# Second block: S5 pairs by couples, and the mixer norm and output product ahead of the S5 drain

## The chip, the cores and the metric

One core of one Trainium2 chip runs the whole program. The metric is device time in microseconds (us) of one execution, lower is better. Engines: PE (TensorE, matmuls), DVE (VectorE), ACT (ScalarE), POOL (GpSimd) and SP (which issues the loads). Each engine works through its own instructions in order; semaphores tie them together.

## The reference

256 tokens of width 1024 go through two blocks. The first (attention, short convolution, a large expert layer) isn't touched. The second puts 16 meta tokens ahead (272 positions in all) and computes:

```
h = layer_norm(concat([meta, x]))
p = h @ w_in + b_in                    # u_s5, q, k, v, o_pre, i_pre, f_pre, g_s5, g_m
# S5: 32 groups of 16 channels, 64 complex states each
state_t = lam_bar * state_(t-1) + b_bar @ u_t ;   y = Re(c @ state) + d * u
z = gelu(y_s5) @ s5_w_glu ;   y_s5 = z[:, :1024] * sigmoid(z[:, 1024:])
# mLSTM: 4 heads, running maximum, numerator over denominator
hm = head_norm(mlstm(silu(conv(q)), silu(conv(k)), v, i_pre, f_pre))
y_m = (sigmoid(o_pre) * hm) @ m_w_out
mix = sigmoid(g_s5) * y_s5 + sigmoid(g_m) * y_m
h = layer_norm(ALPHA * h + mix @ w_o)
out = layer_norm(ALPHA * h + relu(h @ w_up + b_up)^2 @ w_down)
```

## The kernel before, in words

Features stand on the 128 partitions, tokens on the columns. Large products are made in three: each weight tile (128 x 1024) is loaded, rounded to a high part `hi` by ACT (line 189), and its remainder `lo` is made by DVE (line 192); `mm3` (lines 212, 215, 216) multiplies hi by hi, hi by lo and lo by hi. A tile of the input projection (`project`, printed as `pj`) is 24 matmuls. There are three buffers of each of raw, hi and lo.

PSUM has four whole banks for tiles (`bank`), and four `single` banks. `s5_pair(p)` handles two of the 32 groups of S5, 16 pairs in all. Two input matmuls (`bu`, line 1665: real and imaginary part) use 32 rows of PE's array each; rows 32 x (p mod 4). DVE then turns them by the states' angles (six products, lines 1671 to 1676) and scans them (line 1680, `wr` and `wi`), and POOL turns them back (six products, lines 1683 to 1688, of which 1686, `wr`, is printed last). `s5_read(p)` makes the output, two matmuls (`s5y`, line 1699) on 32 columns of the array; four pairs fill one bank, and after the fourth DVE adds `d * u` (`s_y`), and ACT takes the gelu.

The mLSTM has per head `mlstm_head` (`negm`, `qk`, and the weights `m_e`) and `mlstm_sums` (`num`, line 1528, then the statistics `m_st` and `m_ag`). `mlstm_out` takes the denominators and variances of all heads (lines 1542 to 1551, with a root on ACT in `rsqrt`), norms the eight row tiles (four on ACT, line 1556, four on DVE, line 1561), turns them in 16 transposes (`hmT`, line 1571) and multiplies by the output gate (`yin_f`, line 1573).

S5 pairs, gate steps and heads aren't written where they run. They are put in a queue with a cost, `later(cost, fn)`; `pump(budget)`, called after each projection tile, takes items while the budget lasts, and `drain()` takes the rest. Budgets are P_V per tile of values and P_S per gate tile. A scheduler with its own time line then sets the order on each engine, by readiness and by the order of writing. In before the queue holds heads and S5 items mixed; 24 gate tiles (o, gs, gm; `sig0` to `sig2`) are projected with a pump each, then comes the drain, then `mlstm_out`, the gated unit (`glu`, eight tiles), the output product (`ym`, eight tiles) and `w_o`.

Of the kernel before, what the change touches and what calls it, by code (L numbers as in the profile page):

```python
# [18 lines left out]
T = 256  # L19
# [46 lines left out]
P_U, P_V, P_QK, P_S = 0.9, 2.5, 0.6, 2.4  # L66
# [10 lines left out]
K1, K1_BUFS = 272, 12  # L77
# [3 lines left out]
class K:  # L81
# [136 lines left out]
    def after(self, x, y):  # L218
        """The instruction x behind y in the order of their engine."""
# [3 lines left out]
    def rsqrt(self, v):  # L223
        """1 / sqrt(v), with a step of Newton's after the root."""
        nc, (p, n) = self.nc, v.shape
        r, t, h = (self.work(64, "rs_" + x, 3)[0:p, 0:n] for x in "rth")
# [11 lines left out]
    def rms_scale(self, ssq, n, width, eps):  # L238
        v = self.work(64, "rs_v", 3)[:, 0:n]
# [8 lines left out]
    def ln_scale(self, st, p=128):  # L248
        """mean and 1 / sd of rows, from the statistics of their halves."""
# [3 lines left out]
        v = self.work(64, "rs_v", 3)[0:p, 0:1]  # L253
# [3 lines left out]
    def transposed(self, xn, k):  # L257
        """The k-th 128 features of all tokens, in two halves of PSUM banks."""
# [72 lines left out]
    def silu_row_at_once(self, row):  # L331
        """The same with a small load: the tensor engine repeats the row."""
# [9 lines left out]
    def ada_col(self, m, f, ring=None, pool=False, paced=False):  # L342
        """The f-th column of the m-th vector, without its bias."""
# [13 lines left out]
    def ada_gate(self, m, g):  # L357
        """The m-th vector as a row on all partitions."""
# [16 lines left out]
    def modulation(self, m, norm, name, k=0, n=8):  # L375
        """Scale and shift of blocks k.. of the features; m is the vector of shifts, m + 1 that of scales."""
# [30 lines left out]
    def rms_rows(self, x, t, ssq, xn):  # L407
        """x -> x / rms, from the sums of the squares of quarters."""
        nc = self.nc
        s = self.work(64, "rs_s", 3)[:, 0:1]  # L410
# [9 lines left out]
    def add_gated(self, acc, gate, quarter, row):  # L420
        """x1 += acc * gate by quarters of the rows of t, with what follows each of them."""
# [132 lines left out]
    def qkv_load(self, i, per):  # L554
        """The i-th tile of weights of q, or of k and v: that many blocks of 128 features."""
# [19 lines left out]
    def conv_branch(self):  # L575
        """Features on partitions."""
# [351 lines left out]
    def ranks(self, t):  # L928
        """Places among the candidates -> ranks in the two lists that they were made of."""
# [59 lines left out]
    def expert_in(self, j):  # L989
        """The activations of experts j (mod 128); where the gates are there already, times those."""  # L990
# [15 lines left out]
    def gates(self, t0):  # L1006
        """The gates of 8 tokens: onto the activations that are there, and in the places of the others."""
# [48 lines left out]
    def sum_rows(self, acc, n, term, after=None, held=HELD):  # L1056
        """acc[t] = sum of n products; the last ones of t = 0 go before those of t = 1, and those by halves."""
# [43 lines left out]
    def open_lo(self):  # L1101
        """What the second block needs of its own, in the place of the first half of the experts."""
# [26 lines left out]
    def second_block(self):  # L1129
# [22 lines left out]
        for p in range(16):  # L1152
            self.later(2.8, self.s5_pair, p, u)
            if p:
                self.later(0, self.s5_read, p - 1, u)
            for step in steps[2 * p:2 * p + 2]:
                self.later(*step)
        self.later(0, self.s5_read, 15, u)
# [20 lines left out]
        while heads or rest:  # L1179
            for item in (heads.pop(0) if heads else []):  # L1180
                self.later(*item)
            self.queue.extend(rest[:4])
            rest = rest[4:]
        for n, name in enumerate(("b_o", "b_gs", "b_gm")):
            if n == 2:
                sig.append(cb([128, 8, L], "sig2")[:, :, 0:256])
            for c in range(8):
                b = self.project(20 + 8 * n + c, T)
                nc.scalar.activation(out=sig[n][:, c, :], in_=b, func=AF.Sigmoid, bias=self.vec(name, c))
                self.pump(P_S)  # L1190
# [90 lines left out]

    def lead_tiles(self, src):
# [46 lines left out]
    def add_residual(self, acc, h, row):  # L1329
        """x1 = ALPHA * h + acc, by halves of rows, with what follows the rows of t."""  # L1330
# [13 lines left out]
    def norm_row(self, t, st):  # L1344
        """(x - mean) / sd of the rows t of x1, in place of them."""
# [11 lines left out]
    def hold(self, x):  # L1357
        """The parts of the next tiles of weights that are taken on the vector engine come after x."""
# [55 lines left out]
    def if_gates(self):  # L1414
        """log i and log f of the four heads, and what the mixer needs of them, step by step."""
# [122 lines left out]
    def mlstm_out(self, rows, sig_o):  # L1538
# [13 lines left out]
        for h in range(4):  # L1552
            for t in range(2):
                i = 4 * t + h
                if h in NORM_ACT:
                    nc.scalar.activation(
                        out=rows[:, t, h, :], in_=rows[:, t, h, :], func=AF.Identity, scale=r[:, i:i + 1],
                        bias=nb[:, i:i + 1],
                    )
                    continue  # L1560
                nc.vector.tensor_scalar(
                    out=rows[:, t, h, :], in0=rows[:, t, h, :], scalar1=ag[:, i, 0:1], scalar2=r[:, i:i + 1],
                    op0=ALU.subtract, op1=ALU.mult,
                )
        self.tap("hm", rows)
        yin = self.ca([128, 2, 8, 256], "yin", F32R, tag="big", bufs=2)
        for c in range(8):
            b = self.bank("hmT")
            for t in range(2):
                e = (c % 2) * 128  # L1570
                nc.tensor.transpose(b[:, t * 128:t * 128 + 128], rows[:, t, c // 2, e:e + 128], self.ident)
            x = self.f256("yin_f")
            nc.vector.scalar_tensor_tensor(
                out=x, in0=b[:, 0:256], scalar=self.vec("mnorm_g", c), in1=sig_o[:, c, :],
                op0=ALU.mult, op1=ALU.mult,
            )
            self.split_into(yin[:, 0, c, :], yin[:, 1, c, :], x, YIN_ACT)
        return yin[:, 0], yin[:, 1]
# [18 lines left out]
    def s5_rates(self, free):  # L1597
# [12 lines left out]
        # (exp(lam dt) - 1) / lam  # L1610
# [16 lines left out]
        # the factor goes to the output's side: c * factor, its imaginary part negative  # L1627
# [13 lines left out]
    def s5_turns(self, p):  # L1641
        """cos and sin of the states' angles at each step."""
# [14 lines left out]
    def s5_pair(self, p, u):  # L1657
# [186 lines left out]
```

## Time and profile before

| | |
|---|---|
| runs | 1480.24, 1484.26, 1486.38 us; median 1484.26 |
| the profiled execution | span 1485.1 us, all that is timed of it, 0.8 us over the median |
| PE, DVE, ACT, POOL busy | 1418.8, 1129.7, 758.3, 144.7 us |
| loads from memory | 259.5 MB; a tile of 512 KB lands 3.5 us (median) behind its issue |
| chain that ended last | PE 78%, DVE 12%, ACT 4%, DMA 3% |
| the second block | from about 980 us to the end; S5 and mLSTM about 1020 to 1200 |

A row of the time line gives the start, the time from first to last of its instructions, the engine, line, operation, names (out<-in), partitions and columns, and their number; fp32 matmuls of S5 and mLSTM show as two instructions each. In brackets stands the idle time before it and the instruction that ended it. Matmuls overlap in the pipe, so the cost of one is read from its start to the next one's start. The table by stretches has PEclk, the granted clock of PE as a share of full speed.

### The profile page before, as it was taken

What the parts mean: (1) busy time and instruction counts of PE and PEld (TensorE: products, weight loads), DVE (VectorE), ACT (ScalarE), POOL (GpSimd) and SP (SyncE); (2) the same over time, 40 slices, a digit from 0 to 9 for tenths busy, and PEclk for the clock granted to TensorE, in tenths of its full rate; (3) what the DMA queues carried; (4) which work ended last, traced back from release to release, by engine and by line L of the source; (5) the groups of instructions that cost most, each with busy time, mean ns of one, the idle gap of its engine ahead of it and who ended that gap; (6) DMA issues with size and microseconds to landing.
All of it is one profiled execution on the core that took longest, in us unless ns stands there. A gap on an engine that the chain in (4) does not pass through costs nothing.

```text
span 1485.1 us, 24290 instructions
## 1 busy us (share of the span) xinstructions
PE 1418.8 (96%) x9217; PEld 1256.7 (85%) x9217; DVE 1129.7 (76%) x2330; ACT 758.3 (51%) x1292; POOL 144.7 (10%) x128
## 2 busy tenths in 40 slices
PE   6888999999999999999999999999899999999996
PEld 3776899999999999988887788878686799789995
DVE  7888799967788888665566688768799878675556
ACT  3365455544444444455445558745385474455552
POOL 0141000000000000000000000002756510000001
PEclk9998999999999999999999999999899999999999
DMA  9773446554444444555557685553232255366552
GB/s 383 293 267 114 171 149 195 194 174 153 146 139 146 143 146 146 172 189 185 190 192 243 216 270 194 186 187 129 85 128 95 96 193 186 113 200 201 195 186 99
DMA packets 72287, 263.20 MB, mean 177 GB/s; under 512 B 8149, under 2 KB 8533, under 8 KB 71786
## 3 DMA queue, kind: packets, MB, share of 16 engines
q1 hardware_dynamic: 72170, 261.66, 52.2%
q8 instruction: 72, 1.18, 0.3%
q14 instruction: 45, 0.37, 0.1%
HBM read 259.53 MB, written 2.10 MB: 176 GB/s over the span
## 4 chain that ended last, share of the span: by engine, by line
PE 78%; DVE 12%; ACT 4%; DMA 3%; issue 2%; POOL 1%; DVEq 0%; ACTq 0%; POOLq 0%
PE ea L216 8%; PE ea L212 8%; PE ea L215 8%; PE pe L215 7%; PE pe L216 7%; PE pe L212 7%; DVE lo L192 3%; PE gt L1021 2%; PE gt L1022 2%; PE ff L215 2%; PE ff L212 2%; PE ff L216 2%; PE up L216 2%; PE up L215 2%; PE up L212 2%
## 5 line engine op out<-in xcount | busy, mean ns | idle before, releaser
L189 ACT ACTIVATE hi<-raw 128x1024 fp32r<-128x1024 f32 x398 | 419.9, 1055 | 426.0 <-PE ea L215 108.4
L192 DVE TENSOR_TENSOR lo<-raw,hi 128x1024 fp32r<-128x1024 f32 x398 | 488.6, 1229 | 192.8 <-ACT hi L189 190.2
L212 PE MATMUL ea<-h,hi 128*128 128x256 f32 x1024 | 288.5, 282 | 0.8 <-ACT hi L189 0.8
L215 PE MATMUL ea<-h,hi 128*128 128x256 f32 x1024 | 289.1, 283 | 0.0
L216 PE MATMUL ea<-h,lo 128*128 128x256 f32 x1024 | 288.7, 283 | 0.0
L215 PE MATMUL pe<-lo,whi 128*128 128x512 f32 x512 | 201.0, 395 | 0.9 <-DVE lo L192 0.8
L216 PE MATMUL pe<-hi,wlo 128*128 128x512 f32 x512 | 199.0, 394 | 0.0
L212 PEld LDWEIGHTS ea<-h,hi 128*128 128x128 f32 x1024 | 193.7, 189 | 1.0 <-ACT hi L189 1.0
L216 PEld LDWEIGHTS ea<-h,lo 128*128 128x128 f32 x1024 | 193.5, 189 | 0.0
L215 PEld LDWEIGHTS ea<-h,hi 128*128 128x128 f32 x1024 | 193.4, 189 | 0.0
L212 PE MATMUL pe<-hi,whi 128*128 128x512 f32 x512 | 143.6, 395 | 1.1 <-ACT hi L189 1.0
L215 PEld LDWEIGHTS pe<-lo,whi 128*128 128x128 f32 x512 | 96.4, 188 | 24.7 <-DVE lo L192 2.6
L212 PEld LDWEIGHTS pe<-hi,whi 128*128 128x128 f32 x512 | 95.7, 188 | 23.8 <-ACT hi L189 2.2
L216 PEld LDWEIGHTS pe<-hi,wlo 128*128 128x128 f32 x512 | 96.4, 188 | 21.9
L212 PE MATMUL pj<-hT,hi 128*128 128x256 f32 (+1 forms) x328 | 97.6, 297 | 0.0
L215 PE MATMUL pj<-hT,hi 128*128 128x256 f32 (+1 forms) x328 | 95.0, 290 | 2.5 <-DVE hT L208 2.5
L216 PE MATMUL pj<-hT,lo 128*128 128x256 f32 (+1 forms) x328 | 94.4, 288 | 0.0
L212 PEld LDWEIGHTS pj<-hT,hi 128*128 128x128 f32 x328 | 63.6, 194 | 5.7 <-issue 1.9
L216 PE MATMUL up<-h1T,lo 128*128 128x256 f32 x240 | 66.9, 279 | 0.4 <-DVE lo L192 0.4
L212 PE MATMUL up<-h1T,hi 128*128 128x256 f32 x240 | 67.0, 279 | 0.2 <-ACT hi L189 0.2
L215 PE MATMUL up<-h1T,hi 128*128 128x256 f32 x240 | 66.8, 279 | 0.1
L215 PEld LDWEIGHTS pj<-hT,hi 128*128 128x128 f32 x328 | 63.5, 194 | 3.7 <-DVE hT L208 3.1
(471 smaller groups left out, 2765.9 us busy)
## 6 DMA issues: line engine op xcount, KB each, us to landing
raw<-in_u SPq DMA_DIRECT2D x128, 512.0 KB, 3.5
raw<-in_v SPq DMA_DIRECT2D x128, 512.0 KB, 3.5
raw<-in_sC SPq DMA_DIRECT2D x41, 512.0 KB, 3.5
raw<-in_down SPq DMA_DIRECT2D x32, 512.0 KB, 3.5
raw<-in_up SPq DMA_DIRECT2D x30, 512.0 KB, 3.5
s_hi<-in_ada SPq DMA_DIRECT2D x28, 512.0 KB, 5.7
raw<-in_sA SPq DMA_DIRECT2D x17, 512.0 KB, 4.3
s_hi<-in_sA SPq DMA_DIRECT2D x14, 512.0 KB, 6.2
```

Source lines behind the costliest of these rows:

```text
L189: self.last_hi = nc.scalar.activation(out=hi[:, 0:n], in_=raw[:, 0:n], func=AF.Copy)
L192: x = nc.vector.tensor_tensor(out=lo[:, 0:n], in0=raw[:, 0:n], in1=hi.bitcast(F32)[:, 0:n], op=ALU.subtract)
L212: i = mm(out, lhsT=w[0], rhs=x[0], start=first, stop=False)
L215: mm(out, lhsT=w[0], rhs=x[1], start=False, stop=False)
L216: return mm(out, lhsT=w[1], rhs=x[0], start=False, stop=last)
L1021: nc.tensor.matmul(b[:, i0 + i, :], lhsT=oa[:, :, i], rhs=ob[:, :, i], start=True, stop=False)
L1022: nc.tensor.matmul(b[:, i0 + i, :], lhsT=oa[:, :, i], rhs=oc[:, :, i], start=False, stop=True)
```

## The change

S5 goes by couples of pairs. `s5_in(p)` makes the four input matmuls of pairs p and p+1, real parts of both first, so that neighbours in the order use different rows of the array; it takes all four single banks. `s5_pair(p)` keeps only DVE's and POOL's part. `s5_read(p)` reads a couple, four matmuls on different columns. The order in the queue is in(p), pair(p), read(p-2), pair(p+1).

The heads are put ahead of what is left of S5 in the queue's mixture, with a mark behind the last head. After the 16 tiles of the gates o and gs the queue is pumped until the mark. Then comes the norm's scale; each of the eight gm tiles is followed by the norm of a head's rows (every second tile), two transposes and the split of `yin`, and the output product follows at once, with a pump per tile. The drain of S5 and the gated unit stand behind that. `mix` is now made at the end of the gated unit. `yin` takes two other buffers. Budgets change, 14 instead of 12 scratch tiles are used, and the scratch of `rsqrt` is narrower. No arithmetic goes or comes.

```diff
-P_U, P_V, P_QK, P_S = 0.9, 2.5, 0.6, 2.4
+P_U, P_V, P_QK, P_S, P_M = 0.9, 2.2, 0.6, 1.9, 1.9
-K1, K1_BUFS = 272, 12
+K1, K1_BUFS = 272, 14
...
-        r, t, h = (self.work(64, "rs_" + x, 3)[0:p, 0:n] for x in "rth")
+        r, t, h = (self.work(20, "rs_" + x, 3)[0:p, 0:n] for x in "rth")
...
-        for p in range(16):
-            self.later(2.8, self.s5_pair, p, u)
-            if p:
-                self.later(0, self.s5_read, p - 1, u)
-            for step in steps[2 * p:2 * p + 2]:
-                self.later(*step)
-        self.later(0, self.s5_read, 15, u)
+        for p in range(0, 16, 2):
+            self.later(0, self.s5_in, p, u)
+            for i in range(2):
+                self.later(2.8, self.s5_pair, p + i)
+                if p and i == 0:
+                    self.later(0, self.s5_read, p - 2, u)
+                for step in steps[2 * (p + i):2 * (p + i) + 2]:
+                    self.later(*step)
+        self.later(0, self.s5_read, 14, u)
...
-        while heads or rest:
-            for item in (heads.pop(0) if heads else []):
+        while heads:
+            for item in heads.pop(0):
                 self.later(*item)
             self.queue.extend(rest[:4])
             rest = rest[4:]
-        for n, name in enumerate(("b_o", "b_gs", "b_gm")):
-            if n == 2:
-                sig.append(cb([128, 8, L], "sig2")[:, :, 0:256])
+        self.later(0, self.mark)
+        self.queue.extend(rest)
+        self.marked = False
+        for n, name in enumerate(("b_o", "b_gs")):
             for c in range(8):
-                b = self.project(20 + 8 * n + c, T)
-                nc.scalar.activation(out=sig[n][:, c, :], in_=b, func=AF.Sigmoid, bias=self.vec(name, c))
-                self.pump(P_S)
+                self.gate_tile(20 + 8 * n + c, sig[n][:, c, :], name, c)
             if n == 0:
                 self.later(4.5, self.affine_rows, h0, 0)
+        while not self.marked:
+            self.pump(1.0)
+        sig.append(cb([128, 8, L], "sig2")[:, :, 0:256])
+        yin = [cb([128, 8, 256], "yin_" + n, F32R, tag=t) for n, t in (("h", "qkc"), ("l", "v_rows"))]
+        norms = self.mlstm_norm(rows)
+        for c in range(8):
+            self.gate_tile(36 + c, sig[2][:, c, :], "b_gm", c)
+            self.mlstm_out(c, rows, norms, sig[0], yin)
+        for c in range(8):
+            w = [x.rearrange("p (k f) -> p k f", k=8) for x in self.stream(a["mwo"][c])]
+            b = self.bank("ym")[:, 0:256]
+            for k in range(8):
+                self.mm3(b, [x[:, k, :] for x in w], [x[:, k, :] for x in yin], k == 0, k == 7)
+            nc.vector.tensor_tensor(out=sig[2][:, c, :], in0=b, in1=sig[2][:, c, :], op=ALU.mult)
+            self.pump(P_M)
         self.drain()
-        yin = self.mlstm_out(rows, sig[0])
+        mix = self.ca([128, 2, 8, 256], "mix", F32R, tag="big", bufs=2)
...
             nc.vector.tensor_tensor(out=s, in0=zb[1], in1=s, op=ALU.mult)
-            nc.vector.tensor_tensor(out=sig[1][:, c, :], in0=s, in1=sig[1][:, c, :], op=ALU.mult)
-        mix = self.ca([128, 2, 8, 256], "mix", F32R, tag="big", bufs=2)
-        for c in range(8):
-            w = [x.rearrange("p (k f) -> p k f", k=8) for x in self.stream(a["mwo"][c])]
-            b = self.bank("ym")[:, 0:256]
-            for k in range(8):
-                self.mm3(b, [x[:, k, :] for x in w], [x[:, k, :] for x in yin], k == 0, k == 7)
-            s = self.f256("mix_s")
-            nc.vector.tensor_tensor(out=s, in0=b, in1=sig[2][:, c, :], op=ALU.mult)
-            nc.vector.tensor_tensor(out=s, in0=s, in1=sig[1][:, c, :], op=ALU.add)
+            nc.vector.tensor_tensor(out=s, in0=s, in1=sig[1][:, c, :], op=ALU.mult)
+            nc.vector.tensor_tensor(out=s, in0=s, in1=sig[2][:, c, :], op=ALU.add)
             self.split_into(mix[:, 0, c, :], mix[:, 1, c, :], s)
...
+    def s5_in(self, p, u):
+        bu = [[self.single("bu")[:, 0:L] for _ in range(2)] for _ in range(2)]
+        for z in range(2):
+            for i in range(2):
+                r0 = 32 * (p % 4 + i)
+                self.nc.tensor.matmul(
+                    bu[i][z], lhsT=self.bw[r0:r0 + 32, z, p // 4, :], rhs=u[r0:r0 + 32, p // 4, :],
+                    start=True, stop=True, tile_position=(r0, 0),
+                )
+        self.bu = bu
...
     def s5_read(self, p, u):
-        wr, wi = self.s5_x.pop(p)
-        for z, x in enumerate((wr, wi)):
-            nc.tensor.matmul(
-                yb[r0:r0 + 32, :], lhsT=self.cw[:, z, p, :], rhs=x[:, M:L], start=z == 0, stop=z == 1,
-                tile_position=(0, r0),
-            )
-        if p % 4 == 3:
+        xs = [self.s5_x.pop(p + i) for i in range(2)]
+        for z in range(2):
+            for i in range(2):
+                r0 = 32 * (p % 4 + i)
+                nc.tensor.matmul(
+                    yb[r0:r0 + 32, :], lhsT=self.cw[:, z, p + i, :], rhs=xs[i][z][:, M:L], start=z == 0,
+                    stop=z == 1, tile_position=(0, r0),
+                )
+        if p % 4 == 2:
```

Three places show what the scheduler makes of it. A name's number tells tiles apart. On PE, beside a head's products, stand these inputs and reads of S5 before (`wr_11426` and `wi_11427` belong to one pair, as do `bu_11831` and `bu_11832`):

```order
L1699 MATMUL s5y_11633<-wr_11426,s5_cw_8985 32x256
L1699 MATMUL s5y_11633<-wi_11427,s5_cw_8985 32x256
L1665 MATMUL bu_11831<-u_10862,s5_bw_8984 128x272
L1665 MATMUL bu_11832<-u_10862,s5_bw_8984 128x272
L1502 MATMUL qk_11810<-qkc_11447 16x256
L1502 MATMUL qk_11810<-qkc_11447 128x256
L1665 MATMUL bu_11888<-u_10862,s5_bw_8984 128x272
L1665 MATMUL bu_11889<-u_10862,s5_bw_8984 128x272
```

And at such a place now (`bu_12487` and `bu_12488` are one pair, `bu_12489` and `bu_12490` its neighbour, and the four reads are of two pairs):

```order
L1681 MATMUL bu_12489<-u_10862,s5_bw_8984 128x272
L1681 MATMUL bu_12488<-u_10862,s5_bw_8984 128x272
L1681 MATMUL bu_12490<-u_10862,s5_bw_8984 128x272
L1518 MATMUL qk_12419<-qkc_11419 16x256
L1518 MATMUL qk_12419<-qkc_11419 128x256
L1726 MATMUL s5y_12330<-wr_12279,s5_cw_8985 32x256
L1726 MATMUL s5y_12330<-wr_12335,s5_cw_8985 32x256
L1726 MATMUL s5y_12330<-wi_12280,s5_cw_8985 32x256
L1726 MATMUL s5y_12330<-wi_12336,s5_cw_8985 32x256
```

The reads of two pairs now alternate, and so do most inputs; the fourth input of this couple was pulled ahead.

On DVE, this is the end of the heads' statistics and the rows' norm before:

```order
L192 TENSOR_TENSOR lo_12727<-raw_12724,hi_12726 128x1024
L228 RECIPROCAL rs_r_12954<-rs_t_12955 128x8
L229 TENSOR_SCALAR rs_h_12956<-rs_r_12954 128x8
L233 TENSOR_TENSOR rs_t_12955<-rs_r_12954 128x8
L234 TENSOR_TENSOR rs_t_12955<-rs_t_12955,m_var_12948 128x8
L235 SCALAR_TENSOR_TENSOR rs_r_12954<-rs_t_12955,rs_h_12956 128x8
L1551 SCALAR_TENSOR_TENSOR m_nb_12963<-m_ag_11776,rs_r_12954 128x8
L1561 TENSOR_SCALAR m_rows_11772<-m_rows_11772,m_ag_11776,rs_r_12954 128x256 x4
```

And now:

```order
L229 TENSOR_SCALAR rs_h_12702<-rs_r_12700 128x8
L233 TENSOR_TENSOR rs_t_12701<-rs_r_12700 128x8
L1697 TENSOR_TENSOR wr_12655<-wr_12655,t1_12657 128x272
L192 TENSOR_TENSOR lo_12835<-raw_12832,hi_12834 128x1024
L234 TENSOR_TENSOR rs_t_12701<-rs_t_12701,m_var_12694 128x8
L1699 TENSOR_TENSOR t1_12657<-bu_12625,turn_s_9679 128x272
L1704 SCALAR_TENSOR_TENSOR wr_12655<-s5_rad_8993,wr_12655 128x272
L235 SCALAR_TENSOR_TENSOR rs_r_12700<-rs_t_12701,rs_h_12702 128x8
L1700 TENSOR_TENSOR wi_12656<-wi_12656,t1_12657 128x272
L1568 SCALAR_TENSOR_TENSOR m_nb_12709<-m_ag_11750,rs_r_12700 128x8
L1583 TENSOR_SCALAR m_rows_11746<-m_rows_11746,m_ag_11750,rs_r_12700 128x256 x4
L1704 SCALAR_TENSOR_TENSOR wi_12656<-s5_rad_8993,wi_12656 128x272
```

S5's last pair (`wr_12655`, `wi_12656`) now stands among the steps of the norm, with one scan behind it; between the last statistics and the norm there are now eleven products and three scans of S5's pairs 14 and 15 and one `lo`, where there were two products, two scans and one `lo`.

On PE, the transposes before stand in one block behind the last projection tile:

```order
L1571 MATMUL hmT_12974<-mats_85,m_rows_11772 128x128 x2
L1571 MATMUL hmT_12981<-mats_85,m_rows_11772 128x128 x2
L1571 MATMUL hmT_12988<-mats_85,m_rows_11772 128x128 x2
L1571 MATMUL hmT_12995<-mats_85,m_rows_11772 128x128 x2
L1571 MATMUL hmT_13002<-mats_85,m_rows_11772 128x128 x2
L1571 MATMUL hmT_13009<-mats_85,m_rows_11772 128x128 x2
L1571 MATMUL hmT_13016<-mats_85,m_rows_11772 128x128 x2
L1571 MATMUL hmT_13023<-mats_85,m_rows_11772 128x128 x2
```

And now the first one stands here, one projection tile (`pj_12717`) behind the last numerators, with three more inputs and a read between those:

```order
L212 MATMUL pj_12717<-hT_8981,hi_12713 128x256
L215 MATMUL pj_12717<-hT_8981,hi_12713 128x256
L216 MATMUL pj_12717<-hT_8981,lo_12714 128x256
L1726 MATMUL s5y_12650<-wr_12555,s5_cw_8985 32x256
L1726 MATMUL s5y_12650<-wi_12496,s5_cw_8985 32x256
L1726 MATMUL s5y_12650<-wi_12556,s5_cw_8985 32x256
L1726 MATMUL s5y_12650<-wr_12631,s5_cw_8985 32x256
L1590 MATMUL hmT_12745<-mats_85,m_rows_11746 128x128
L212 MATMUL pj_12758<-hT_8981,hi_12754 128x256
L215 MATMUL pj_12758<-hT_8981,hi_12754 128x256
L216 MATMUL pj_12758<-hT_8981,lo_12755 128x256
```

The read of pair 14 (`wr_12631`) and the first transpose stand ahead of the next tile; the reads of pair 15 follow behind that tile and two more transposes.

## Rows read from the trace of the kernel before

**Rows 1.** The page, busy time of each engine.

```profile
PE 1418.8 (96%) x9217; PEld 1256.7 (85%) x9217; DVE 1129.7 (76%) x2330; ACT 758.3 (51%) x1292; POOL 144.7 (10%) x128
```

**Rows 2.** Stretches: S5 and mLSTM; gated unit and output product (header first).

```profile
core 0: us, PE busy (x) PEld busy (x) DVE busy (x) ACT busy (x) POOL busy (x), PEclk, DMA share, GB/s
1010.00:1200.00 190.00, 179.62 (x1137) 144.78 (x1138) 166.35 (x309) 105.34 (x158) 105.49 (x106) 0.95 0.35 118
...
1219.05:1264.60 45.55, 45.55 (x386) 45.55 (x386) 38.41 (x70) 20.57 (x28) 0.00 (x0) 1.00 0.53 174
```

**Rows 3.** Waits of PE, 985 to 1290: us in total, times, longest.

```profile
PE s5y L1699 <- POOL wr L1686: 5.5, 3, 4.0
...
PE bu L1665 <- DVE wi L1674: 1.6, 1, 1.6
```

**Rows 4.** Time line of PE, the first read of S5 and what follows.

```profile
1049.80 1.06 PE L1699 MATMUL s5y<-wr,s_cw 128*32 128x256 f32 x2 [4.02 <-POOL wr L1686]
...
1051.65 0.60 PE L212 MATMUL pj<-hT,hi 128*128 128x272 f32 x1
```

**Rows 5.** Stretches at half clock (columns as in rows 2).

```profile
1050.00:1054.00 4.00, 4.00 (x14) 2.71 (x13) 0.22 (x1) 0.00 (x0) 4.00 (x6) 0.50 0.26 103
...
1148.00:1156.00 8.00, 8.00 (x21) 4.92 (x20) 4.24 (x14) 0.77 (x2) 4.34 (x6) 0.50 0.20 68
```

**Rows 6.** Time line of PE, inputs of S5 and the next instruction.

```profile
1030.76 1.18 PE L1665 MATMUL bu<-u,s_bw 32*128 32x272 f32 x4
1031.87 0.28 PE L1320 MATMUL vr<-mats,vt 128*16 128x128 f32 x1
...
1138.96 1.19 PE L1665 MATMUL bu<-u,s_bw 32*128 32x272 f32 x6
1140.08 0.62 PE L1699 MATMUL s5y<-wr,s_cw 128*32 128x256 f32 x2
```

**Rows 7.** Time line of PE, reads of S5 and their neighbours.

```profile
1132.74 0.28 PE L216 MATMUL pj<-hT,lo 128*128 128x256 f32 x1
1132.95 0.62 PE L1699 MATMUL s5y<-wr,s_cw 128*32 128x256 f32 x2
...
1133.93 0.39 PE L212 MATMUL pj<-hT,hi 128*128 128x256 f32 x1
...
1163.40 0.40 PE L1699 MATMUL s5y<-wr,s_cw 128*32 128x256 f32 x1
1163.40 0.60 PE L1502 MATMUL qk<-qkc 128*16 128x256 f32 x2
...
1163.95 0.70 PE L1502 MATMUL qk<-qkc 128*128 128x256 f32 x2
```

**Rows 8.** Time line of PE, the block of transposes.

```profile
1215.39 2.23 PE L1571 MATMUL hmT<-mats,m_rows 128*128 128x128 f32 x14
1218.66 0.44 PE L1571 MATMUL hmT<-mats,m_rows 128*128 128x128 f32 x2 [1.04 <-DVE yin_f L1573]
1219.05 0.39 PE L212 MATMUL glu<-yg,hi 128*128 128x256 f32 x1
```

**Rows 9.** Time line of DVE, from the last statistics to the norm.

```profile
1185.88 0.41 DVE L1535 BATCH_NORM_STATS2 m_st<-m_rows 128x6 f32<-128x256 f32 x1
...
1186.30 0.40 DVE L1675 TENSOR_TENSOR t<-bu,turn_s 128x272 f32<-128x272 f32 x1
1186.62 0.71 DVE L1680 TENSOR_TENSOR_SCAN wr<-s_rad,wr 128x272 f32<-128x272 f32 x1
...
1189.42 1.21 DVE L192 TENSOR_TENSOR lo<-raw,hi 128x1024 fp32r<-128x1024 f32 x1
...
1193.40 1.91 DVE L1561 TENSOR_SCALAR m_rows<-m_rows,m_ag,rs_r 128x256 f32<-128x256 f32 x4
```

**Rows 10.** Time line of POOL, first and last products of two pairs.

```profile
1039.49 1.10 POOL L1683 TENSOR_TENSOR t<-wi,turn_s 128x272 f32<-128x272 f32 x1 [21.46 <-DVE wi L1680]
...
1049.71 0.75 POOL L1683 TENSOR_TENSOR t<-wi,turn_s 128x272 f32<-128x272 f32 x1
...
1053.31 0.76 POOL L1686 TENSOR_TENSOR wr<-wr,t 128x272 f32<-128x272 f32 x1
```

More of the change, by code (lines that the diff above doesn't have):

```diff
@@ L238, in rms_scale @@
     def rms_scale(self, ssq, n, width, eps):
-        v = self.work(64, "rs_v", 3)[:, 0:n]
+        v = self.work(20, "rs_v", 3)[:, 0:n]
         self.nc.vector.tensor_scalar(
@@ L252, in ln_scale @@
         nc.vector.bn_aggr(out=ag[0:p], in_=st[0:p])
-        v = self.work(64, "rs_v", 3)[0:p, 0:1]
+        v = self.work(20, "rs_v", 3)[0:p, 0:1]
         nc.vector.tensor_scalar(out=v, in0=ag[0:p, 1:2], scalar1=1e-5, scalar2=None, op0=ALU.add)
@@ L409, in rms_rows @@
         nc = self.nc
-        s = self.work(64, "rs_s", 3)[:, 0:1]
+        s = self.work(20, "rs_s", 3)[:, 0:1]
         nc.vector.tensor_reduce(out=s, in_=ssq[:, 4 * t:4 * t + 4], axis=AX.X, op=ALU.add)
@@ L1280, in second_block, with mark, gate_tile @@
         self.add_residual(acc, h1, last)
+    def mark(self):
+        self.marked = True
+    def gate_tile(self, i, out, name, c):
+        b = self.project(i, T)
+        self.nc.scalar.activation(out=out, in_=b, func=AF.Sigmoid, bias=self.vec(name, c))
+        self.pump(P_S)
     def lead_tiles(self, src):
@@ L1536, in mlstm_sums, with mlstm_norm @@
             nc.vector.bn_aggr(out=self.ag[:, 4 * t + h, :], in_=st)
-    def mlstm_out(self, rows, sig_o):
+    def mlstm_norm(self, rows):
         nc, ag = self.nc, self.ag
@@ L1551, in mlstm_out @@
         nc.vector.scalar_tensor_tensor(out=nb, in0=ag[:, :, 0], scalar=-1.0, in1=r, op0=ALU.mult, op1=ALU.mult)
[L1552 to L1558, printed above, removed]
-                    )
[L1560 to L1563, printed above, removed]
-                )
@@ L1565, in mlstm_out @@
[L1565 to L1575, printed above, removed]
-            )
-            self.split_into(yin[:, 0, c, :], yin[:, 1, c, :], x, YIN_ACT)
@@ L1578, in mlstm_out @@
-        return yin[:, 0], yin[:, 1]
+        return r, nb
+    def mlstm_out(self, c, rows, norms, sig_o, yin):
+        nc, ag, h = self.nc, self.ag, c // 2
+        r, nb = norms
+        for t in range(2) if c % 2 == 0 else ():
+            i = 4 * t + h
+            if h in NORM_ACT:
+                nc.scalar.activation(
+                    out=rows[:, t, h, :], in_=rows[:, t, h, :], func=AF.Identity, scale=r[:, i:i + 1],
+                    bias=nb[:, i:i + 1],
+                )
+                continue
+            nc.vector.tensor_scalar(
+                out=rows[:, t, h, :], in0=rows[:, t, h, :], scalar1=ag[:, i, 0:1], scalar2=r[:, i:i + 1],
+                op0=ALU.subtract, op1=ALU.mult,
+            )
+        b = self.bank("hmT")
+        for t in range(2):
+            e = (c % 2) * 128
+            nc.tensor.transpose(b[:, t * 128:t * 128 + 128], rows[:, t, h, e:e + 128], self.ident)
+        x = self.f256("yin_f")
+        nc.vector.scalar_tensor_tensor(
+            out=x, in0=b[:, 0:256], scalar=self.vec("mnorm_g", c), in1=sig_o[:, c, :],
+            op0=ALU.mult, op1=ALU.mult,
+        )
+        self.split_into(yin[0][:, c, :], yin[1][:, c, :], x, YIN_ACT)
@@ L1655, in s5_turns, with s5_pair @@
         nc.scalar.activation(out=cn, in_=fr, func=AF.Sin, scale=-TWO_PI, bias=self.half_pi)
-    def s5_pair(self, p, u):
+    def s5_in(self, p, u):
[8 more added lines that the diff above has]
+        self.bu = bu
+    def s5_pair(self, p):
         nc = self.nc
         tt = nc.vector.tensor_tensor
-        r0 = 32 * (p % 4)
         cn, sn = (x[:, p, :] for x in self.turn)
-        bu = [self.single("bu")[:, 0:L] for _ in range(2)]
-        for z in range(2):
-            nc.tensor.matmul(
-                bu[z], lhsT=self.bw[r0:r0 + 32, z, p // 4, :], rhs=u[r0:r0 + 32, p // 4, :], start=True, stop=True,
-                tile_position=(r0, 0),
-            )
+        bu = self.bu[p % 2]
         e = self.f272
@@ L1691, in s5_read @@
     def s5_read(self, p, u):
-        nc, r0 = self.nc, 32 * (p % 4)
+        nc = self.nc
         stt = nc.vector.scalar_tensor_tensor
-        wr, wi = self.s5_x.pop(p)
         if p % 4 == 0:
@@ L1697, in s5_read @@
         yb = self.yb
-        for z, x in enumerate((wr, wi)):
-            nc.tensor.matmul(
-                yb[r0:r0 + 32, :], lhsT=self.cw[:, z, p, :], rhs=x[:, M:L], start=z == 0, stop=z == 1,
-                tile_position=(0, r0),
-            )
-        if p % 4 == 3:
+        xs = [self.s5_x.pop(p + i) for i in range(2)]
[5 more added lines that the diff above has]
+                    stop=z == 1, tile_position=(0, r0),
+                )
+        if p % 4 == 2:
             c = p // 4
```

## Prediction

> **What bounds the kernel now.** I read the engines' line of the page first. TensorE (PE) is busy for 1418.8 of 1485.1 us and VectorE (DVE) for 1129.7 [rows 1], so time is won where PE idles, runs at half clock, or uses a small part of its array. Then the table by stretches: in 1010 to 1200 us, where projection tiles, state-space pairs (S5) and mLSTM heads run mixed, PE is busy for 179.6 of 190 us at a mean granted clock of 0.95 and DVE for 166.4, that is 88% [rows 2]. Here PE is the bound with DVE close behind, so a wait of PE on DVE easily appears. In the gated unit and the output product (1219.05 to 1264.60) PE is full: 16 tiles in 45.55 us are 2.85 us a tile [rows 2]. Then the waits of PE over the block's front: 5.5 us for the last GpSimd (POOL) product of a pair, 1.6 us for DVE's `wi` [rows 3]. The timeline shows the largest, 4.02 us ahead of the first read, and that read then takes 1.85 us to the next matmul [rows 4], against 0.98 at full clock [rows 7]. The clock rows say why: the granted clock falls from 2.4 to 1.2 GHz (0.50) at 1050 to 1054 and at 1148 to 1156 [rows 5], each time behind an idle gap of PE and some small matmuls. At full speed these two stretches would have been shorter by 2.0 and 4.0 us.
>
> All sums below are against the profiled span of 1485.1 us. The median of the runs is 1484.3, 0.8 us below it, so I subtract the sum from 1484.3.
>
> **Inputs by couples.** The 32 input matmuls stay. Two on the same 32 rows go one behind the other: a pair, 4 instructions, needs 1.11 us [rows 6], 0.555 a matmul. Three matmuls (6 instructions) of two pairs, on different rows, needed 1.12 us to the next instruction [rows 6] where three in line would take 1.66, so neighbours overlap. Counting neighbours in the two orders, the 32 matmuls fill 31 slots before and 23 after (the scheduler pulls several couples apart): 8 x 0.555 = 4.4 us, all on PE. Bounds: 0 (no overlap) and -4.4; I take -4, as the row shows overlap nearly whole.
>
> **Reads by couples.** A pair's read takes 0.98 us from start to the next [rows 7], of which some 0.06 is the switch; 0.46 a matmul. In the row at 1163.40, a read on 32 columns and a `qk` product on 16 columns start in the same hundredth, and two of each are over in 0.55 us [rows 7], where the two reads alone need 0.46. So column tiles overlap too. By the order, 32 slots become 18: 14 x 0.46 = 6.4 us. Bounds 0 and -6.4; I take -5.5. The Trainium skill, "TensorE: Matmul & The Clock Gate", Part 3 (Measured speedup vs the span model), gives three column tiles 2.38 times the speed of one; an estimate from that is 1.6 for two, and the 14 couples of 0.92 us would save 4.8 us. No row here times two reads side by side; by this page the sum would be 0.7 us smaller in gain.
>
> **Fewer changes between whole array and parts.** A part's matmul begins 0.21 us behind the start of the last whole one (1132.74 to 1132.95) [rows 7], where the next whole one would follow in 0.12 (2.85 over 24); I take the same for the way back. The order has 120 such changes before, 110 after: 10 x 0.1 = -1 us; bounds 0 and -1.
>
> **Transposes among the gate tiles.** Before, 16 transposes stand in one block, 1215.39 to 1219.05: 3.66 us with 1.04 of waiting [rows 8]. Between gate tiles each costs about its issue, 0.1 us, 1.7 in all: -2 us (0 to -3.7).
>
> **The early waits.** The first read now stands three tiles later in the order, so the 4.02 us wait mostly goes, and with it its 2.0 us at half clock. What is late next is the POOL chain of the second pair of the couple: it ends at 1054.07 in the trace of before [rows 10], 4.3 us behind the first read, well inside three tiles of 2.85. The two other waits for POOL (1.5 us) and the one for `wi` (1.6) [rows 3], with 4.0 us of clock behind the last [rows 5], may go or move: a couple now needs all four single banks free, so an input waits for DVE's last read of the couple before. Bounds: -13 (all go: 5.5, 1.6 and 6.0 of clock) and +4 (each is as long as the longest of before, but for the clock); I take -5, the first wait and half its clock, as that row is the one that the order moves.
>
> **The new place: mixer norm ahead of the S5 drain.** This is the dearest term. Before, between the last statistics of the heads (1185.88) and the norm of the rows (1193.40) DVE takes 7.5 us [rows 9], two products and two scans of S5 among it (0.32 each from start to start, 0.63 a scan: 1.9), so the chain alone is 5.6; the 1.21 us `lo` lies in its wait for ScalarE's (ACT) root. PE doesn't wait for it, since ten projection tiles (28 us) stand before the first transpose. After, DVE's order holds eleven products, two scans ahead of the end (a third lies in the wait for the root) and one `lo` in the same place: 11 x 0.32 + 2 x 0.63 + 1.21 = 6.0 us, so the norm begins 5.6 + 6.0 = 11.6 us behind the last numerator, and the first transpose, one norm (0.5) and a hand-over later, 12.3 behind. PE has between them only two slots of inputs (1.1), one tile (2.85), five reads in four slots (1.8) and switches: 6.0 us. It waits about 6.3 us, first at the read of pair 14, then at the transpose; the next tiles' hi and lo are there, but stand behind it on PE. After one more tile and transposes (3.1 us) the reads of pair 15 wait: its last scan comes behind four norms (1.91 us [rows 9]) and then six POOL products, 4.4 us where POOL is alone (1049.71 to 1054.07) and 10.2 where it isn't (1039.49 to 1049.71) [rows 10]. Last norm at 13.5, scan to 14.2, POOL to 18.6 or 24.4; PE is there at 15.4: 3.2 or 9.0 us. I take 3.7, near the pair that has POOL alone, since DVE's long tile work is over there. Together 10 us; bounds 0, if DVE runs these early, and 15, if POOL takes 10.2. Behind gaps of this size the clock fell by half in rows 5; I add 3 us, the mean of the two losses there (0 to 4).
>
> **Gated unit and output product.** The same 16 tiles and arithmetic. DVE had 2.4 us a tile on average [rows 2]; now a gated tile has all four elementwise steps and the split, 1.2 + 4 x 0.42 + 0.29 = 3.2 us against PE's 2.85, 8 x 0.35 = 2.8 us behind at the end. Three buffers of weight parts absorb most, and the last part of `mix` is needed only by the last eighth of `w_o`: +0.5, bounds 0 and 3. The smaller budgets per tile, the narrower scratch tiles and the later loads move nothing that PE waits for in these rows; the FFN's first weights, loaded later into the buffer of the low parts, have eight tiles (23 us) to arrive. If that cover were gone, PE would wait for one landing, 3.5 us by the table of the profile.
>
> Sum: -4 - 5.5 - 1 - 2 - 5 + 10 + 3 + 0.5 = -4 us, so 1480 us.
>
> **The rivals.** *No new wait* (A): the scheduler's place for the norm is as good in the trace as in its plan, because DVE has run ahead and S5's last pairs are done before the last numerator. For it: PE's waits of S5 sum to only 7.1 us in the whole stage now [rows 3], under the same kind of order. Against: the pairs' own DVE rows stand behind the last statistics in the order. The 10 and the 3 go: -4 - 13 = -17, of which short waits may keep one: about 1468.
> *DVE becomes the bound* (B), the case on the other side: couples shorten PE's 190 us by ten, DVE's 166 us stay, and every input of a couple waits until DVE has emptied four banks. Then the early waits stay (0 in place of -5), POOL is contended at pair 15 (15 in place of 10), and the gated tiles keep their whole lag (3 in place of 0.5): -4 + 5 + 5 + 2.5 = +8.5: 1493. It decides once DVE is over some 92% busy in this stretch, 166 us over the 180 that PE needs.
> *The tiles of the array don't overlap between couples* (C), so that the change doesn't do what it says: the 9.5 us of inputs and reads stay away: -4 + 9.5 = +5.5, 1490. For it: the rows that show overlap are of unlike operations, with other operands. Against: they start in the same hundredth. The Trainium skill, "TensorE: Matmul & The Clock Gate", Part 3 (The mechanism), says that weight loads overlap running matmuls only where the row group differs. Reads share all rows, so by this rule theirs would stay in line; the pair at 1163.40, which shares the rows too, speaks against it here.
>
> **Chances and range.** My sum 0.42, A 0.30, B 0.15, C 0.13. Half a per cent, 7.4 us, is about what a measurement of this kernel tells from no change: faster is below 1476.9, slower above 1491.7. Of my sum a quarter ends under 1476.9; C ends mostly within; B mostly above. Faster 0.40, same 0.42, slower 0.18. From the bounds of the unknown terms my sum's own range is 1472 to 1488; with A below and most of B above, eight in ten lie in 1464 to 1494.
>
> **What would show it.** Right: two inputs of a couple starting within 0.05 us of each other, and a couple's read over in about 1.1 us where two pairs took 1.96; no 4 us wait at the first read; PE waiting some 6 us in sum at the read of pair 14 and the first transpose, and 3 to 5 at that of pair 15, with a granted clock of 0.5 behind it; no block of 16 transposes. Wrong: reads of a couple 0.46 apart (C); PE's waits for `bu` over 5 us in sum or DVE over 92% (B); the first transpose without idle time before it (A). A time under 1464 would mean that I overrated the new wait and underrated the clock; above 1494, that S5 waits for banks at each couple.

## The result, and the profile after

The changed kernel takes 1493.72 us (median, 1491.31 to 1498.51), the kernel before 1484.82 in the runs beside it: 1.0067 times as long, interval 1.0047 to 1.0086. The time lies at the upper end of the range; the forecast was a gain of 4 us, and it is a loss of 9.

The engines' line of the page after: PE and DVE do as much as before [rows 1], in 9.5 us more.

```profile
PE 1416.7 (95%) x9217; PEld 1257.2 (84%) x9217; DVE 1127.5 (75%) x2330; ACT 758.5 (51%) x1293; POOL 144.9 (10%) x128
```

The stretch 1030 to 1210 us, first of before, then of after (columns as in rows 2):

```profile
1030.00:1210.00 180.00, 171.95 (x1099) 138.96 (x1098) 155.35 (x288) 102.15 (x151) 100.42 (x104) 0.94 0.35 118
```

```profile
1030.00:1210.00 180.00, 158.16 (x1066) 130.48 (x1065) 154.77 (x293) 103.22 (x154) 100.08 (x104) 0.93 0.33 110
```

DVE is as busy as before, 86%, and PE idles more. These two stretches don't hold the same work, as the second block begins 5.8 us later in the profile after. From its first projection tile to the FFN's first tile the matmuls are the same 1840, first before, then after:

```profile
1007.30:1296.70 289.40, 275.80 (x1840) 234.02 (x1838) 237.28 (x436) 155.79 (x230) 107.34 (x107) 0.96 0.39 131
```

```profile
1013.10:1304.00 290.90, 264.75 (x1840) 229.08 (x1838) 234.26 (x436) 155.87 (x231) 107.26 (x107) 0.96 0.39 131
```

PE is busy for 11 us less and idle for 12.5 us more (13.6, then 26.2): what the couples freed is waited away. The waits of PE, 985 to 1300, answer to rows 3:

```profile
PE s5y L1726 <- POOL wr L1710: 8.1, 4, 7.1
PE vr L1336 <- ACT vt L1329: 4.9, 2, 4.1
PE bu L1681 <- DVE wi L1698: 4.0, 2, 3.3
...
PE hmT L1590 <- DVE m_rows L1583: 0.4, 1, 0.4
```

**Couples on the array.** The time line of PE after, against rows 6 and 7:

```profile
1029.39 0.73 PE L1681 MATMUL bu<-u,s_bw 32*128 32x272 f32 x4
1030.05 0.40 PE L212 MATMUL pj<-hT,hi 128*128 128x272 f32 x1
...
1066.29 0.63 PE L1726 MATMUL s5y<-wr,s_cw 128*32 128x256 f32 x4
1066.75 0.60 PE L1726 MATMUL s5y<-wi,s_cw 128*32 128x256 f32 x4
1067.28 0.17 PE L1482 MATMUL gT<-mats,g_i 4*16 4x4 f32 x1
```

Two inputs of different pairs are over in 0.66 us, where two of one pair took 1.11. Four reads of a couple are over in 0.99, where one pair's two took 0.98: the second pair is free. The estimate from the Trainium skill's ratio ("TensorE: Matmul & The Clock Gate", Part 3, Measured speedup vs the span model) was 1.6 times the speed for two column tiles; here it is 2.0, and the measurement decides. From each start on PE to the next, idle time left out, inputs sum to 14.1 us (17.6 before) and reads to 11.2 (18.2; between 16.6 and 18.2 in the profiles that keep the order of before, as some reads fall into half clock).

**The new place.** DVE after, from the last statistics to the norm (rows 9 before: 7.5 us), and to the last scan of S5:

```profile
1186.94 0.41 DVE L1551 BATCH_NORM_STATS2 m_st<-m_rows 128x6 f32<-128x256 f32 x1
...
1199.27 1.37 DVE L1583 TENSOR_SCALAR m_rows<-m_rows,m_ag,rs_r 128x256 f32<-128x256 f32 x4
1200.56 0.71 DVE L1704 TENSOR_TENSOR_SCAN wi<-s_rad,wi 128x272 f32<-128x272 f32 x1
```

And PE there:

```profile
1198.33 1.06 PE L1726 MATMUL s5y<-wr,s_cw 128*32 128x256 f32 x2 [7.12 <-POOL wr L1710]
1199.82 0.45 PE L1590 MATMUL hmT<-mats,m_rows 128*128 128x128 f32 x1 [0.42 <-DVE m_rows L1583]
...
1205.80 0.40 PE L1726 MATMUL s5y<-wr,s_cw 128*32 128x256 f32 x1 [0.56 <-POOL wr L1710]
...
1207.51 0.39 PE L212 MATMUL pj<-hT,hi 128*128 128x256 f32 x1 [0.65 <-DVE s_y L1733]
```

12.3 us in place of 7.5, and four waits of 8.75 us together. The granted clock is 1.2 GHz behind the longest, so the tile between is slow:

```profile
1200.00:1202.00 2.00, 2.00 (x11) 2.00 (x11) 1.27 (x3) 1.46 (x3) 0.65 (x1) 0.50 0.03 8
1202.00:1204.00 2.00, 2.00 (x12) 2.00 (x11) 0.00 (x0) 0.00 (x0) 2.00 (x4) 0.50 0.00 0
```

**The early wait moved.** The read that waited 4.02 us [rows 4] no longer does. The next instruction in line, `vr`, which takes value rows that ACT makes as `vt`, waits as long at the same place of the work:

```profile
1056.52 0.38 PE L1336 MATMUL vr<-mats,vt 128*16 128x128 f32 x1 [4.10 <-ACT vt L1329]
```

ACT and DVE there, in order of time:

```profile
1053.43 1.28 ACT L1478 ACT_TABLE_LOAD   x1
1054.72 0.43 ACT L1478 ACTIVATE g_x<-g_x 4x272 f32<-4x272 f32 x1
1055.06 1.04 ACT L189 ACTIVATE hi<-raw 128x1024 fp32r<-128x1024 f32 x1
1056.01 0.83 ACT L1329 ACTIVATE vt<-pj,vecs 128x272 f32<-128x272 f32 x2
```

```profile
1052.72 0.27 DVE L1340 COPY v_rows<-vr 16x128 f32<-16x128 f32 x1
1052.92 0.28 DVE L1477 TENSOR_SCALAR g_x<-g_x 4x272 f32<-4x272 f32 x1
1053.12 1.21 DVE L192 TENSOR_TENSOR lo<-raw,hi 128x1024 fp32r<-128x1024 f32 x1
1054.26 0.70 DVE L1704 TENSOR_TENSOR_SCAN wi<-s_rad,wi 128x272 f32<-128x272 f32 x1
```

`vt` stands on ACT behind the exponent of the gate steps, and that behind DVE's row `g_x`; DVE has no gap from 1038.8 to 1055.0.

**And 8 us outside the changed stretch.** From the first expert tile to the second block's first projection, which the change doesn't touch, the profile after takes 804.6 us against 798.4; from the FFN's first tile to the end 190.6 against 188.4. Only 1.5 us of the loss lie between. Both parts run the same instructions, in the FFN in the same order; in the first part two neighbours on PE and some rounding steps of ACT and DVE have changed places. That this isn't the cause is shown by the second kernel below, which keeps that order and has the time back.

### The profile page after: what moved, and what is told of

Same layout as the page of the kernel before. It is cut to its first block, busy times and chain, and to the rows that moved or that the text cites. A ratio compares the mean times of both kernels' runs of the same rounds, so it can differ in the third digit from the quotient of the medians.

```text
span 1494.6 us, 24282 instructions
## 1 busy us (share of the span) xinstructions
PE 1416.7 (95%) x9217; PEld 1257.2 (84%) x9217; DVE 1127.5 (75%) x2330; ACT 758.5 (51%) x1293; POOL 144.9 (10%) x128
```

## The experiments

A ratio is to the kernel before in the same runs, with its 95% interval. Medians of before were 1484.7 to 1485.3 us.

**Addresses alone.** The narrower scratch and the two added scratch tiles move all long-lived operands 224 bytes down. The first kernel moves them so and changes no engine's order:

```diff
-        r, t, h = (self.work(64, "rs_" + x, 3)[0:p, 0:n] for x in "rth")
+        r, t, h = (self.work(20, "rs_" + x, 3)[0:p, 0:n] for x in "rth")
...
-        ang = self.wk.tile([128, 2, 32], F32, name="ang", tag="ang", bufs=1)
+        ang = self.wk.tile([128, 608], F32, name="ang", tag="ang", bufs=1)[:, 0:64].rearrange("p (t f) -> p t f", t=2)
```

> The kernel before, every engine's order unchanged, only the addresses: the scratch of rsqrt is 20 wide and one other scratch tile larger, so that the transposed activations and all that lies behind them sit 224 bytes lower, as in the changed kernel. Theory (layout): the 6 us that the changed kernel loses outside the touched stretch come from these addresses: 1490 to 1492 us, with matmuls of the FFN's first product 116 to 117 ns apart in place of 113 to 114. Rival (scatter between executions): no difference, 1483 to 1487 us.

1493.58 us, 1.0069 (1.0045 to 1.0093). No instruction is added, and the loss is that of the whole change. One tile of the FFN's first product in the time line of PE (line 212 starts it, line 216 ends it; 24 matmuls), in the kernel before:

```profile
1402.91 0.28 PE L212 MATMUL up<-h1T,hi 128*128 128x256 f32 x1
...
1405.54 0.28 PE L216 MATMUL up<-h1T,lo 128*128 128x256 f32 x1
```

And with the addresses moved:

```profile
1402.46 0.28 PE L212 MATMUL up<-h1T,hi 128*128 128x256 f32 x1
...
1405.18 0.27 PE L216 MATMUL up<-h1T,lo 128*128 128x256 f32 x1
```

2.63 us from the first start to the last, then 2.72, with PE busy and at full clock in both. The duration shown, 0.28, tells nothing of it; starts do. The execution profiled here took 1487.26 us, with a start up to the first expert tile that was 5.9 us quicker than in the profile of before; the two parts outside the changed stretch still take 802.4 and 190.7 us in it, where before has 798.4 and 188.4.

The second kernel takes the changed one and moves the operands back:

```diff
-        ang = self.wk.tile([128, 2, 32], F32, name="ang", tag="ang", bufs=1)
+        ang = self.wk.tile([128, 120], F32, name="ang", tag="ang", bufs=1)[:, 0:64].rearrange("p (t f) -> p t f", t=2)
```

> The changed kernel, every engine's order unchanged, with one scratch tile 224 bytes larger, so that the long-lived operands sit where they sat before. Theory (layout): 1486 to 1489 us, 6 less than the changed kernel. Rival (scatter): as the changed kernel, 1492 to 1495 us.

1487.77 us, 1.0011 (0.9995 to 1.0027), and the two parts are back at 799.0 and 188.3 us. So of 8.9 us some 6 are addresses, and the edit by itself costs 2.5 by the medians, 1.6 by the ratio, no change that can be measured.

**Couples alone**, at the addresses of before (the functions of the couples, the queue's order for them, `K1_BUFS` 14 and the narrower scratch of `rsqrt` as in the diff of the change, with `ang` enlarged as above; the rest as before):

> Couples alone: inputs and reads of S5 by couples, 14 scratch tiles, the long-lived operands at the addresses of before; the norm, the transposes and the output product stay behind the drain, and the budgets are those of before. Theory (the move is what costs, couples save 11 us on the array and lose up to 5 in early waits): 1474 to 1480 us. Rival (DVE is the bound in the stretch, so the array's time is handed back in waits): 1483 to 1488 us.

1482.50 us, 0.9973 (0.9956 to 0.9991). Between theory and rival: 2.7 us gained of some 9 saved on the array. The waits, 985 to 1300:

```profile
PE bu L1665 <- DVE wi L1682: 4.7, 2, 3.5
PE num L1530 <- DVE m_e L1517: 2.8, 1, 2.8
...
PE s5y L1710 <- POOL wr L1694: 2.2, 2, 1.8
```

**The move alone**, single pairs, budgets of the change, addresses of before:

```diff
-        for p in range(0, 16, 2):
-            self.later(0, self.s5_in, p, u)
...
+        for p in range(16):
+            self.later(2.8, self.s5_pair, p, u)
```

> The move alone: S5 by single pairs as before, at the addresses of before; norm, transposes and output product ahead of the S5 drain, with the changed budgets. Theory (the move costs 14 us of waits and clock at the last pairs and gives 3 back at the transposes): 1493 to 1497 us. Rival (the waits at the last pairs come from the couples' late inputs): 1483 to 1487 us.

1493.08 us, 1.0065 (1.0042 to 1.0088), at the lower end of the theory's range. The wait is there without any couple, now all of it at the transpose:

```profile
PE hmT L1588 <- DVE m_rows L1581: 6.6, 1, 6.6
PE s5y L1715 <- POOL wr L1702: 4.6, 3, 4.0
```

**What the address does.** Three more kernels with the order of before. 96 bytes lower, from one scratch name 56 wide in place of 64:

```diff
-        s = self.work(64, "rs_s", 3)[:, 0:1]
+        s = self.work(56, "rs_s", 3)[:, 0:1]
```

> The kernel before with one scratch name 8 elements narrower, so that all behind it, the transposed activations among it, sits 96 bytes lower; every engine's order unchanged. Theory (alignment: what counts is the address modulo 64; it is 32 for the moving operands before, and 0 where matmuls were slow): 0 again, so slow as with 224 bytes, 1490 to 1494 us, FFN matmuls 116 to 120 ns apart. Rival (some other property of the 224-byte shift, such as the distance to other tiles): the time of before, 1483 to 1487 us.

192 bytes lower, from 48 in place of 64:

> The kernel before with one scratch name 16 elements narrower: all behind it 192 bytes lower, the address modulo 64 stays 32. Theory (alignment): the time of before, 1483 to 1487 us, FFN matmuls 113 to 114 ns apart. Rival (any shift hurts): 1490 to 1494 us.

And all from the weight tiles on 32 bytes higher:

```diff
-        self.ones = self.const.tile([128, 128], F32, name="ones")
+        self.ones = self.const.tile([128, 136], F32, name="ones")[:, 0:128]
```

> The kernel before with a constant 32 bytes longer at the front, so that the weight tiles and the moving operands both sit 32 bytes higher, all at 0 modulo 64. If the address of the moving operand alone decides: slow, 1490 to 1495 us. If it decides by its place relative to the weight tiles: the time of before, 1483 to 1487 us.

1493.08 (1.0061, 1.0041 to 1.0081), 1486.15 (1.0010, 0.9988 to 1.0031) and 1484.28 us (1.0004, 0.9987 to 1.0022). From the starts in the traces I take the median time of a tile of three products, from the first of its 24 starts to the last, in ns (for `up` of the 27 tiles whose 24 records stand in one row):

| | expert input `ea` | FFN `up` | output product `ym` |
|---|---|---|---|
| before | 2722 | 2624 | 2709 |
| 224 lower | 2734 | 2720 | 2723 |
| 96 lower | 2735 | 2756 | 2757 |
| 192 lower | 2721 | 2752 | 2760 |
| all 32 higher | 2725 | 2624 | 2607 |
| changed | 2734 | 2719 | 2757 |
| changed, moved back | 2722 | 2624 | 2757 |

`ea`, the largest, follows the theory: slow when weight tiles and moving operand differ by 32 modulo 64, at its old pace when both move. `up` at 192 lower contradicts it (2752), so the address modulo 64 isn't all. Nor is the distance all: with both moved by 32, `ea` and `up` keep their pace and `ym` goes from 2709 to 2607, and at one and the same address `ym` takes 2709 in the kernel before and 2607 in a later one, whose transposes stand elsewhere. Shown is that placement alone costs up to 8 us here, with every engine's order the same; the rule behind it stays open.

**The new wait covered.** The changed kernel at the old addresses, with transposes three gate tiles later and the last couple's read behind the fourth gm tile:

```diff
-        for c in range(8):
-            self.gate_tile(36 + c, sig[2][:, c, :], "b_gm", c)
-            self.mlstm_out(c, rows, norms, sig[0], yin)
+        for c in range(11):
+            if c < 8:
+                self.gate_tile(36 + c, sig[2][:, c, :], "b_gm", c)
+            if c == 3:
+                self.drain()
+                self.s5_read(14, u)
+            if c >= 3:
+                self.mlstm_out(c - 3, rows, norms, sig[0], yin)
```

> The changed kernel at the addresses of before, with the last S5 couple's read behind the fourth gm tile and each head's transposes three gate tiles later; DVE's order up to the norm unchanged. Theory (the new wait at pair 14's read and the first transpose, 8.8 us, and its clock, 5.1 us, is what the move costs, and three tiles cover it): 13 us less than the 1487.8 of the changed kernel at these addresses, 1473 to 1477 us. Rival (DVE's arrears there move on and PE waits for them later): 1483 to 1488 us.

1481.48 us, 0.9978 (0.9961 to 0.9995): 6.3 us less by the medians, 4.9 by the ratios, half of what was expected or less. The waits, 1184 to 1214:

```profile
PE pj L212 <- ACT sig L1299: 2.1, 1, 2.1
PE s5y L1732 <- POOL wr L1716: 1.3, 2, 1.1
PE pj L212 <- DVE s_y L1741: 0.7, 1, 0.7
```

8.75 us became 4.1. The largest of them, 2.1 us, shows what was overlooked: on ACT the norms wait for DVE's chain, and the sigmoid that empties a gate tile's bank stands behind them, so PE waits for the bank:

```profile
1193.10 2.08 ACT L1582 ACTIVATE m_rows<-m_rows,m_nb,rs_r 128x256 f32<-128x256 f32 x4 [3.18 <-DVE m_nb L1572]
1195.08 1.04 ACT L189 ACTIVATE hi<-raw 128x1024 fp32r<-128x1024 f32 x1
1196.03 0.45 ACT L1299 ACTIVATE sig<-pj,vecs 128x256 f32<-128x256 f32 x1
```

**DVE relieved.** The changed kernel at the old addresses with the sine half of DVE's turn of each pair left out:

```diff
         tt(out=wr, in0=bu[0], in1=cn, op=ALU.mult)
-        tt(out=t1, in0=bu[1], in1=sn, op=ALU.mult)
-        tt(out=wr, in0=wr, in1=t1, op=ALU.add)
         tt(out=wi, in0=bu[1], in1=cn, op=ALU.mult)
-        tt(out=t1, in0=bu[0], in1=sn, op=ALU.mult)
-        tt(out=wi, in0=wi, in1=t1, op=ALU.subtract)
```

> The changed kernel at the addresses of before with four of DVE's eight operations of each S5 pair left out (both products with the sine and both sums, so the input is not fully turned); all PE, POOL and ACT work stays. It takes some 16 x 1.4 = 22 us from DVE in the stretch. Theory (the waits that took the place of the early ones, 4.0 us at the value rows and 4.4 at the inputs, and most of the 8.8 at pair 14 and the transposes are DVE's arrears): PE's waits between 1035 and 1210 fall from about 20 us to under 8, and the time from 1487.8 to 1471 to 1476 us. Rival (POOL's six products and ACT's order set these waits): less than 4 us gained, 1484 to 1488 us.

1472.13 us, 0.9912 (0.9887 to 0.9936): 15.6 us less, with the same work on PE and POOL. The time is the forecast one, but not by its terms alone: the waits, 1030 to 1215, fall from 21.5 us to 14, not to 8:

```profile
PE hmT L1590 <- DVE m_rows L1583: 4.9, 1, 4.9
PE s5y L1722 <- POOL wr L1706: 3.2, 1, 3.2
...
PE bu L1681 <- DVE wr L1695: 1.3, 1, 1.3
PE vr L1336 <- ACT vt L1329: 1.1, 1, 1.1
```

The two early ones fell from 4.8 and 4.1 to 1.1 and 1.3: those are DVE's arrears. The norm still has no cover. From the first projection tile to the FFN's first tile it is 276.7 us in place of 292.5, and only 7.5 us of that are idle time of PE; for the rest the same matmuls keep PE busy for less, at a granted clock of 0.98 in place of 0.95. So the waits cost about twice their own length here.

**A better version.** Couples alone, with the transposes two by two behind the tiles of the gated unit:

```diff
             nc.vector.tensor_tensor(out=sig[1][:, c, :], in0=s, in1=sig[1][:, c, :], op=ALU.mult)
+            self.head_turned(c, rows, sig[0], yin)
```

> Couples alone (1482.5 us) with one more edit: the 16 transposes stand two by two behind the tiles of the gated unit in place of one block; the norm of the rows and the S5 drain stay where they were. Theory (interleaved transposes give 2 us back and nothing new waits, as the norm is long done): 1479 to 1482 us. Rival (DVE, with 3.0 us of work for a gated tile against PE's 2.85, hands it back): 1482 to 1485 us.

1479.59 us, 0.9949 (0.9930 to 0.9969), as the theory has it, and faster than both kernels. The 3.66 us block [rows 8] is gone and nothing new waits for the norm.

On top of it, the gate steps thinned out:

```diff
-                for step in steps[2 * (p + i):2 * (p + i) + 2]:
+                for step in steps[p + i:p + i + 1]:
```

> As the kernel with transposes among the gated unit, and the five steps of the i and f gates one to a pair in place of two. Theory (the early waits, 4.0 us at whichever PE instruction comes next, are DVE's arrears behind two pairs and the gate steps at 1038 to 1055): with half the steps there the wait and its clock, some 5 us, go: 1474 to 1478 us. Rival (the arrears are only spread over the next pairs, DVE being near its limit in the whole stretch): no difference, 1479 to 1483 us.

1482.24 us, 0.9978 (0.9964 to 0.9992), no better: the rival. From 1030 to 1215 PE waits for 13 us in both. The inputs `bu` wait for 2.8 us in place of 4.7 and the numerators `num` for 2.0 in place of 4.3, but `vr` waits for `vt` for 3.1 in place of 0.8 and the reads for 4.0 in place of 2.1; the arrears go elsewhere. And the same version with all 32 bytes higher:

> As the kernel with transposes among the gated unit, with weight tiles and operands all 32 bytes higher, where the output product's matmuls took 113 in place of 118 ns. Theory (their place relative to each other decides the pace): 1 us less, 1478 to 1481 us. Rival (slow, as with the operands alone moved): 1486 us or more.

1479.93 us, 0.9961 (0.9946 to 0.9977): as without it. The expected microsecond isn't there, since `ym` already takes 2607 ns a tile in the version that it is compared with.

## Why the prediction was wrong

| term | predicted | measured | from |
|---|---|---|---|
| inputs | -4 | -3.5 | starts on PE, 17.6 to 14.1 |
| reads, with fewer changes | -6.5 | -7.0 | 18.2 to 11.2 |
| transposes | -2 | -2.3 | 2.6 and a wait of 1.0, to 1.4 |
| early waits | -5 | +1.5 | waits 7.9 to 13.1, clock 3.7 less |
| new place, waits | +10 | +8.75 | four waits |
| new place, clock | +3 | +2.9 | 5.9 us at half clock |
| gated unit, output product | +0.5 | +0.4 | 45.5 to 45.9 |
| addresses | 0 | +6 to +8 | moved back; moved alone |

Without the last row the measured terms add up to +0.8 us, and the changed stretch took 1.5 us more. So two steps failed, and they are about equally large.

**The step that failed** is the sentence that priced "the smaller budgets per tile, the narrower scratch tiles and the later loads" at nothing. I looked for a wait that they could cause and found none; they cause none. The narrower scratch, with the two added scratch tiles, moves the moving operands of the large products, and the same matmuls then start further apart, by the medians 0.5 ns each in the experts' first product and 4 ns in the FFN's. That is 6 to 8 us in place of nothing. No row of before shows it, and I set no bound. It makes the loss one that can be measured: with the operands moved back the kernel is at 1.0011, which is still not the gain of 4 us that was forecast.

**The early waits** were the second step that failed, priced at -5 us and measured at +1.5. I asked what the read would wait for, found it ready in time (as it was) and let the wait go. But the whole front from 1038 on waited for DVE, and the next instruction inherited the 4 us; that DVE is what it waits for is shown by the run that relieves DVE. My bound of +4 held it; I took a value on the wrong side of zero. The rows in hand, DVE at 88% [rows 2], spoke for rival B, and B was right in this term. The signs that I had set for it didn't come: `bu` waited for 4.3 us in sum, under the 5, and DVE was at 86%, under the 92; they were set too high. B's figure, 1493, is the measured time by accident, as 6 us of it are addresses, which B doesn't have.

**The new place** was right in mechanism and size: 12.3 us of DVE's chain against 11.6 worked out. One row was misjudged: I gave 6.3 us to pair 14 and the first transpose and 3.7 to pair 15, and it was 7.5 and 1.2, since POOL was alone and PE late, at half clock. What the wait was worth was less sure than it looked: covering it gave 6.3 us back, and not the 11.7 of wait and clock: 4.1 us of waits stayed, half of them because ACT hands on the same delay.

**Couples** overlap, so rival C is refuted, and their gain on the array came as worked out. Alone they bring 2.7 us, as PE then waits for DVE; that relieving DVE frees the rest is shown for the changed kernel alone. Rival A is refuted by the four waits.

## What to carry to other kernels

A change of a scratch tile's size is a change of every address behind it: time it alone with the order unchanged, and compare the distance between starts of matmuls in stretches that the change doesn't touch. A wait is gone only if the engine that is late does less or something else stands in between; ask which instruction is next in line on the waiting engine and what it needs. Chains that end in a norm want cover on every engine that they pass, the one that empties the banks too.

## What the runs showed of the hardware

The pace of equal matmuls depends on placement: 24 matmuls of 256 columns took 2624 to 2756 ns from first start to last in the FFN, at full clock and without idle time, 114 to 120 ns each. Two reads on neighbouring 32-column tiles cost as much as one (four in 0.99 us, two in 0.98). Time from the program's start to the first expert tile varied between executions, from 203.0 to 208.9 us in kernels that are equal up to there but for addresses, so profiles are better compared from a later mark than from zero.
